# A change in five places of a hybrid encoder layer: conv-norm stores by GpSimd, its means as fp32r products, the ninth tile of values in two products, the first weight load by ScalarE

## The chip, the cores and the metric

One core of a Trainium2 chip runs the whole layer. TensorE (PE in the profile) multiplies, VectorE (DVE), ScalarE (ACT) and GpSimd (POOL) compute element by element, and SyncE (SP) issues most of the transfers. Each engine works through its own list of instructions in order. An instruction waits for the semaphores of what it needs, and everything behind it on that engine waits with it. The metric is the device time of one execution in microseconds (us); lower is better. A profiled execution also gives the span from the first to the last instruction.

## The reference, cut to what matters

A layer takes 1024 frames of a prompt and 32 frames of a running stream, 1056 rows in all, with 1024 features each:

```
p = x @ w_in                    # split into: GLU pair | q | k | v | forget logits | gate logits
u = a * sigmoid(b)              # GLU pair, 512 channels
y = causal depthwise conv, width 31, over u
y = silu(LayerNorm over the 512 channels of (y + b_dw))    # the conv norm
y_conv = y @ w_conv_out
o = forgetting attention(q, k, v, cumulated log forget gates), 8 heads of 64
m = sigmoid(g_conv) * y_conv + sigmoid(g_attn) * (o @ w_attn_out)
x1 = LN1(alpha * x + m @ w_o)
x2 = LN2(alpha * x1 + relu(x1 @ w_up)^2 @ w_down)
```

The new rows of u, k, v and log f are outputs too. Everything is fp32.

## The kernel before, in words

**Products.** An fp32 number is split into a high part (a copy in the type fp32r, made by ScalarE) and a low part (the difference, made by VectorE). A dense product is then three products of the parts: high by high, high by low, low by high (`dense` and `mm3`, recorded by `mm`, L206). Weights come in halves through a ring `raw`, and are split into `whi` and `wlo` (class `Weights`: `load`, `split`, `take`). The rows of x are kept split in `xh0..7` and `xl0..7`, with 128 features on the partitions and 1056 columns each, worked on as three chunks of 352 columns.

**Start.** `x_stream` loads weights (`raw`) and x (`xr`, two features' tiles a piece) by the SP queue and splits them. TensorE first runs 19 products that nobody reads (`keep_warm`, tile `ps_warm`), and some more between the first products of `ps_glub`, where it would wait for x.

**Stages.** First the GLU pairs (`glua`, `glub`), then the values (`ps_v`: nine tiles of 128 rows, in two halves of 260 columns; the ninth covers rows 928 to 1055 and only its last 32 are used), then q and k, then 16 tiles of gates (`ps_g`, 24 products to a chunk). Six of the gate tiles run in the first part of the kernel, which has eight PSUM banks for them. The other ten are filler in the attention stage, which has two banks for them (`bbank`). ScalarE empties a bank by copying it to `gt`; the copy is then stored to `g_s`.

**The conv norm** (`conv`) runs beside this on VectorE and ScalarE: 31 taps for each of four channel tiles, then sums of the channel tiles (`lns`), means and variances by a product with the constant matrix `mean_c` (`ps_mu_c`, `ps_var_c`, three blocks of 362 columns), `rstd_c` and a reciprocal for each block, and then twelve pieces (three blocks by four channel tiles). A piece is scaled (VectorE), passed through a sigmoid (ScalarE, `csig`), multiplied (VectorE), split into high (ScalarE, `csh`) and low (VectorE, `csl`), and both parts are stored to `s_s` by the SP queue. The third block's rows are cut in two, so its stores are two each. The y products read `s_s` much later, in the attention stage.

**Order.** Engines' lists come from running this code with an estimate of every instruction's time (class `Issue`): `conv` is a generator that is advanced between groups of products when its next step is due by that estimate. `MARGIN` says how long a product with `mean_c` waits after its sums. At the end of the first part, `I.flush()` writes out whatever of `conv` is left.

**Attention.** Its tiles reuse the memory of the first part. Head 0 is loaded by GpSimd's queue (`load_head`, `queue = nc.gpsimd if h == 0`), behind three memsets of GpSimd's (`k2`, `q2`, called `k` and `q` in the profile); other heads are loaded by SP. The first scores, `ps_s`, need all of head 0's k and q. After them the kernel goes on with gates, attention, the y products, w_o and its norm, the feed-forward products (`ps_u`, `ps_d`, `ps_dn`) and the last norm.

## Time and profile before

| what | value |
| --- | --- |
| median of 3 runs | 1446.77 us (1445.07 to 1447.04) |
| the profiled execution's own time | 1445.13 us |
| its span | 1443.0 us |
| TensorE busy | 1427.9 us, 99% of the span |
| VectorE busy | 1121.0 us, 78% |
| ScalarE busy | 679.1 us, 47% |
| GpSimd busy | 124.5 us, 9% |
| gates tiles before attention | 245.3 to 318.1 us |
| the first scores | 334.31 us |

All times of instructions below count from the span's start. A row of the timeline gives start, length, engine, line of the kernel, operation, what is written `<-` what is read, how many, and in brackets how long the engine had been idle and what ended that. The chain of waits follows the work that ended last, in order of time.

### The profile page before, as it was taken

The numbers are of one execution on the slowest core, as the hardware profiler recorded it, in microseconds if no ns is written. First come the engines' busy times: TensorE is split into PE (matmuls) and PEld (weight loads), VectorE is DVE, ScalarE is ACT, GpSimd is POOL, SyncE is SP. The second block draws the span as 40 slices with busy tenths as digits, with TensorE's granted clock in tenths as the row PEclk, the third lists the DMA queues.
The fourth block names the chain that finished last, engine by engine and source line by source line (L and its number), as shares of the span: only waits on it lengthen the run. The fifth ranks groups of instructions, "written<-read, shape, count | busy, mean of one in ns | idle before, by whom it ended". The sixth has DMA issues, their size and how long they took to land.

```text
span 1443.0 us, 28013 instructions
## 1 busy us (share of the span) xinstructions
PE 1427.9 (99%) x10643; PEld 1406.3 (97%) x10643; DVE 1121.0 (78%) x1927; ACT 679.1 (47%) x1426; POOL 124.5 (9%) x183
## 2 busy tenths in 40 slices
PE   9999999999999999999999999999999999999996
PEld 8999999999999999999999999999999999999996
DVE  6999899875666555756697888889876799889668
ACT  5113433455656556533245666676657323322134
POOL 0000000023455533000000000000000000000000
PEclk9999999999999999999999999999999999999998
DMA  7125454278455557425243348766689999894212
GB/s 247 48 61 160 159 171 167 85 244 233 120 150 147 155 146 260 152 93 182 85 138 120 131 152 295 249 241 230 228 283 342 340 321 330 270 324 179 67 45 77
DMA packets 157441, 267.91 MB, mean 186 GB/s; under 512 B 22680, under 2 KB 81272, under 8 KB 157308
## 3 DMA queue, kind: packets, MB, share of 16 engines
q1 hardware_dynamic: 156492, 264.24, 55.0%
q0 software_dynamic: 544, 1.59, 0.5%
q8 instruction: 84, 1.38, 0.4%
q14 instruction: 49, 0.40, 0.1%
q10 hardware_dynamic: 272, 0.29, 0.1%
HBM read 168.29 MB, written 97.74 MB: 184 GB/s over the span
## 4 chain that ended last, share of the span: by engine, by line
PE 97%; DVE 1%; ACT 0%; DMA 0%; issue 0%; SPq 0%; DVEq 0%
PE ps_u L206 18%; PE ps_d L206 17%; PE ps_g L206 13%; PE ps_o L206 6%; PE ps_dn L206 6%; PE ps_up L206 5%; PE ps_v L206 4%; PE ps_yc L206 3%; PE ps_k L206 3%; PE ps_glua L206 3%; PE ps_q L206 3%; PE ps_glub L206 3%; PE ps_yo L206 3%; PE ps_s L206 3%; PE ps_pv L206 2%; PE ps_tr L210 2%
## 5 line engine op out<-in xcount | busy, mean ns | idle before, releaser
L235 DVE SCALAR_TENSOR_TENSOR ca<-u,prm,ca 128x1086 f32<-128x1086 f32 x120 | 161.8, 1348 | 2.4
L206 PE MATMUL ps_g<-xh,whi 128*128 128x352 f32 x384 | 131.8, 343 | 0.0
L218 ACT ACTIVATE swhi<-s 128x512 fp32r<-128x512 f32 x100 | 61.9, 624 | 148.2 <-DVE s L227 139.8
L206 PE MATMUL ps_g<-xh,wlo 128*128 128x352 f32 x384 | 123.8, 322 | 0.0
L206 PE MATMUL ps_g<-xl,whi 128*128 128x352 f32 x384 | 121.5, 322 | 0.0
L206 PE MATMUL ps_u<-tl,swhi 128*128 128x264 f32 x416 | 118.4, 285 | 0.0
L206 PE MATMUL ps_u<-th,swhi 128*128 128x264 f32 x416 | 118.2, 284 | 0.0
L206 PE MATMUL ps_u<-th,swlo 128*128 128x264 f32 x416 | 118.2, 284 | 0.0
L218 ACT ACTIVATE whi<-raw 128x512 fp32r<-128x512 f32 (+1 forms) x120 | 69.7, 624 | 68.6 <-PE ps_glua L206 21.8
L227 DVE TENSOR_TENSOR tl<-ps_tr,th 128x512 fp32r<-128x512 f32 (+2 forms) x96 | 51.5, 553 | 60.1 <-ACT th L218 59.4
L206 PE MATMUL ps_d<-hu_h,swhi 128*128 128x264 f32 x480 | 93.0, 285 | 0.0
L206 PE MATMUL ps_d<-hu_l,swhi 128*128 128x264 f32 x480 | 92.8, 285 | 0.0
L218 ACT ACTIVATE r<-r 128x528 f32<-128x528 f32 (+1 forms) x120 | 73.9, 615 | 37.8 <-DVE r L227 35.5
L227 DVE TENSOR_TENSOR r<-r,ps_u 128x528 f32<-128x528 f32 x91 | 62.7, 701 | 29.5 <-PE ps_u L206 29.5
L227 DVE TENSOR_TENSOR wlo<-raw,whi 128x512 fp32r<-128x512 f32 (+1 forms) x100 | 64.9, 687 | 23.5 <-ACT whi L218 21.6
L206 PEld LDWEIGHTS ps_u<-th,swhi 128*128 128x128 f32 x416 | 78.3, 188 | 0.0
L206 PEld LDWEIGHTS ps_u<-th,swlo 128*128 128x128 f32 x416 | 78.3, 188 | 0.0
L206 PEld LDWEIGHTS ps_u<-tl,swhi 128*128 128x128 f32 x416 | 78.2, 188 | 0.0
L227 POOL TENSOR_TENSOR acc<-acc,lnrest 128x288 f32<-128x288 f32 x4 | 3.0, 796 | 856.7 <-ACT lnrest L218 856.7
L206 PEld LDWEIGHTS ps_d<-hu_h,swhi 128*128 128x128 f32 x480 | 74.6, 189 | 0.3 <-issue 0.2
L206 PEld LDWEIGHTS ps_d<-hu_l,swhi 128*128 128x128 f32 x480 | 74.6, 189 | 0.0
L206 PEld LDWEIGHTS ps_g<-xh,whi 128*128 128x128 f32 x384 | 72.7, 189 | 0.8
(424 smaller groups left out, 5005.5 us busy)
## 6 DMA issues: line engine op xcount, KB each, us to landing
h_s<-sp SPq DMA_DIRECT2D x84, 528.0 KB
raw<-in_w_in_dram SPq DMA_DIRECT2D x64, 256.0 KB
hu_h<-h_s SPq DMA_DIRECT2D x30, 528.0 KB
hu_l<-h_s SPq DMA_DIRECT2D x30, 528.0 KB
sraw<-in_w_up_dram SPq DMA_DIRECT2D x52, 256.0 KB
hu<-h_s SPq DMA_DIRECT2D x24, 528.0 KB
sraw<-in_w_ds_dram SPq DMA_DIRECT2D x48, 256.0 KB
g_s<-gt SPq DMA_DIRECT2D x48, 176.0 KB
```

The costliest lines, as they stand in the source:

```text
L206: self.nc.tensor.matmul(ps, lhsT=w, rhs=x, start=start, stop=stop)
L210: self.nc.tensor.transpose(ps, x, ident)
L218: self.nc.scalar.activation(out, in_, func, **kw)
L227: (self.nc.vector if eng == "dve" else self.nc.gpsimd).tensor_tensor(out, a, b, op)
L235: self.nc.vector.scalar_tensor_tensor(out, a, s, b, op0, op1)
```

## The change

- The two parts of a conv-norm piece now lie in one tile `cs` (two parts by 362 columns, a ring of four), and are stored by one transfer each (two for the third block), issued by GpSimd. `s_s` is laid out to match.
- The sums of the conv norm are split into fp32r parts too, in tiles of the same ring: one more ScalarE copy and one more VectorE subtraction for each of the six sums. A mean is then two fp32r products with `mean_c`, now of type fp32r, in place of one fp32 product.
- The ninth tile of values takes only the 32 rows it needs, with the high and low parts side by side as 64 columns of the stationary operand (`xs`, written by 16 ScalarE copies). One product with `whi` and one with `wlo` for each of the eight feature tiles takes the place of three; ScalarE and VectorE then add the two halves of the result.
- The first weight half is loaded by ScalarE's queue, ahead of its first activation; the second weight half is split after the second piece of x, not after the first; the fill-in products among the first `ps_glub` products become 2 and 1, from 5 and 2.

```
-    s_s = [tc.dram_tile([NJ, P, T], F32, name=f"s{i}_s") for i in range(2)]
+    s_s = tc.dram_tile([NJ, 2, P, T], F32, name="s_s")
...
-    act(tiny, eps, AF.Sigmoid)
...
-            W.load()
+            W.load(nc.scalar)
+            act(tiny, eps, AF.Sigmoid)
             issue()
             issue()
             W.load()
...
             W.split()
             for i in range(4 * NCH):
-                if i == 1:
+                if i == 2:
                     W.split()
...
-        mean_c = pv_.tile([P, P], F32, name="mean_c")
-        nc.gpsimd.memset(mean_c, 1.0 / C_CONV)
+        mean_c = pv_.tile([P, P], F32R, name="mean_c")
+        nc.gpsimd.memset(f32(mean_c), 1.0 / C_CONV)
...
-                    keep_warm({1: 5, 3: 2}.get(k, 0))
+                    keep_warm({1: 2, 3: 1}.get(k, 0))
...
                 for t in src[2:]:
                     tt(a, a, t, ADD)
-                return a
+
+                parts = pv_.tile([P, 2, CC], F32R, tag="cs", bufs=4, name=f"cs_{kind}{c}")
+                parts = [parts[:, 0], parts[:, 1]]
+                act(parts[0], a, AF.Copy)
+                tt(parts[1], a, f32(parts[0]), SUB)
+                return parts
...
-                mm(mu, mean_c, sums[c], True, True)
+                for i, a in enumerate(sums[c]):
+                    mm(mu, mean_c, a, i == 0, i == 1)
...
-                mm(var, mean_c, sums[c], True, True)
+                for i, a in enumerate(sums[c]):
+                    mm(var, mean_c, a, i == 0, i == 1)
...
-                    hi, lo = (pv_.tile([P, CC], F32R, tag=x, bufs=4, name=f"{x}{c}_{j}") for x in ("csh", "csl"))
+                    both = pv_.tile([P, 2, CC], F32R, tag="cs", bufs=4, name=f"cs{c}_{j}")
+                    hi, lo = both[:, 0], both[:, 1]
                     act(hi, z, AF.Copy)
                     tt(lo, z, f32(hi), SUB)
-                    for dst, src in ((s_s[0][j], hi), (s_s[1][j], lo)):
-                        if c < 2:
-                            dma(dst[:, blocks[c]], src)
-                        else:
-                            e = SEQ - 2 * CC
-                            dma(dst[:, 2 * CC:SEQ], src[:, :e])
-                            dma(dst[:, SEQ:T], src[:, CC - DEC:])
+                    dst = s_s[j].rearrange("i p t -> p i t")
+                    if c < 2:
+                        dma(dst[:, :, blocks[c]], both, nc.gpsimd)
+                    else:
+                        e = SEQ - 2 * CC
+                        dma(dst[:, :, 2 * CC:SEQ], both[:, :, :e], nc.gpsimd)
+                        dma(dst[:, :, SEQ:T], both[:, :, CC - DEC:], nc.gpsimd)
...
+        xs = pa.tile([P, 2, CH], F32R, tag="xr", bufs=XB, name="xs").rearrange("p a x -> p (a x)")
+        xs = xs[:, :2 * KD * DEC].rearrange("p (k x) -> p k x", k=KD)
+        for k in range(KD):
+            for i, t in enumerate((xh, xl)):
+                act(xs[:, k, i * DEC:(i + 1) * DEC], f32(t[k][:, SEQ:T]), AF.Copy)
...
+                    for n, (x, *w2) in enumerate(terms):
+                        for i, w in enumerate(w2):
+                            mm(ps[0:2 * DEC], x, w, n == i == 0, n == KD - 1 and i == 1)
+                        I.service()
+                    both = pa.tile([P, 2, CH], F32, tag="xr", bufs=XB, name=f"xs_{half}")
+                    both = [both[:DEC, i, :VW] for i in range(2)]
+                    for i in range(2):
+                        act(both[i], ps[i * DEC:(i + 1) * DEC], AF.Copy)
+                    tt(both[0], both[0], both[1], ADD)
```

The change also moves instructions, since the estimates of the conv norm are other ones. A row of an engine's list gives the line, the operation, and what is written and read.

TensorE, around the third product of variances, before (`ps_g_0_85` is the tenth of the 18 chunks of gates that come before attention):

```order
L206 MATMUL ps_g_0_85_3132<-xh_144,whi_2756 128x352
L206 MATMUL ps_g_0_85_3132<-xl_152,whi_2756 128x352
L206 MATMUL ps_g_0_85_3132<-xh_144,wlo_2757 128x352
L206 MATMUL ps_var_c_86_3151<-lns_v_3061,mean_c 128x362
L206 MATMUL ps_g_0_85_3132<-xh_145,whi_2756 128x352
```

and in the changed kernel (`ps_g_1_89` is the fourteenth chunk):

```order
L206 MATMUL ps_g_1_89_3281<-xh_138,whi_2859 128x352
L206 MATMUL ps_g_1_89_3281<-xl_146,whi_2859 128x352
L206 MATMUL ps_g_1_89_3281<-xh_138,wlo_2860 128x352
L206 MATMUL ps_var_c_90_3288<-cs_v_3153,mean_c 128x362 x2
L206 MATMUL ps_g_1_89_3281<-xh_139,whi_2859 128x352
```

Before, 234 products of gates stand ahead of it; now 318 do. The first scores stand behind 534 products of gates in both, and 432 of these are the 18 chunks.

ScalarE, from the copy of the eighteenth chunk (`ps_g_2_94`) on, before (`gt_0_3617` copies the first chunk of the attention stage's gates, `ps_g_0_3592`, and the third of these chunks, `ps_g_2_3648`, writes the bank that this copy empties):

```order
L218 ACTIVATE gt_2_3515<-ps_g_2_94_3478 128x352
L218 ACTIVATE whi_3518<-raw_3250 128x512
L218 ACTIVATE whi_3518<-raw_3254 128x512
L218 ACTIVATE csig_3_3529<-ca_261,prm 128x362
L218 ACTIVATE csh_2_3532<-ca_260 128x362
L218 ACTIVATE csh_3_3541<-ca_261 128x362
L218 ACT_TABLE_LOAD
L218 ACTIVATE tiny<-eps 128x1
L218 ACTIVATE gt_0_3617<-ps_g_0_3592 128x352
```

and in the changed kernel, the last rows ahead of the same `gt_0_3617`:

```order
L218 ACTIVATE csig_1_3517<-ca_258,prm 128x362
L218 ACTIVATE cs_0_3520<-ca_257 128x362
L218 ACTIVATE csig_2_3526<-ca_259,prm 128x362
L218 ACTIVATE cs_1_3529<-ca_258 128x362
L218 ACTIVATE csig_3_3535<-ca_260,prm 128x362
L218 ACTIVATE cs_2_3538<-ca_259 128x362
L218 ACTIVATE cs_3_3544<-ca_260 128x362
L218 ACT_TABLE_LOAD
L218 ACTIVATE tiny<-eps 128x1
L218 ACTIVATE gt_0_3617<-ps_g_0_3592 128x352
```

Before, two high parts of pieces (`csh_2`, `csh_3`) stood between the copy of the eighteenth chunk and `gt_0_3617`. Now seven do: the four of the third block shown here, and the last three of the second block, which follow the eighteenth chunk's copy and its two `whi`.

GpSimd, between its first memsets and the second head's, before:

```order
L827 MEMSET k_0_3563 64x1088
L829 MEMSET q_0_3565 64x1024
L830 MEMSET q_0_3565 2x1024
L201 DMA k_0_3568<-kh_s 64x1024 x2
L201 DMA q_0_3569<-qh_s 64x1024
L201 DMA q_0_3569<-ql_s 64x1024
L201 DMA k_0_3563<-kl_s 64x1024
L201 DMA k_0_3563<-c_s 2x8x128
L201 DMA q_0_3565<-qh_s 64x1024
L201 DMA q_0_3565<-c_s 2x8x128
```

and in the changed kernel, from the last four stores to the first of head 0's loads:

```order
L201 DMA s_s<-cs_2_3538 128x2x300
L201 DMA s_s<-cs_2_3538 128x2x32
L201 DMA s_s<-cs_3_3544 128x2x300
L201 DMA s_s<-cs_3_3544 128x2x32
L852 MEMSET k_0_3563 64x1088
L854 MEMSET q_0_3565 64x1024
L855 MEMSET q_0_3565 2x1024
L201 DMA k_0_3568<-kh_s 64x1024 x2
```

Sixteen stores now stand in GpSimd's list ahead of the memsets and of head 0's loads.

More of the change, by code (lines that the diff above doesn't have):

```diff
@@ L327, in __init__, with load @@
             self.engine, self.limit = "dve", NWO + 1
-        def load(self):
+        def load(self, queue=None):
             i = len(self.raw)
@@ L334, in load @@
             n = w.shape[1] // 2
-            dma(self.raw[i][:, :n], w[:, i % 2 * n:(i % 2 + 1) * n])
+            dma(self.raw[i][:, :n], w[:, i % 2 * n:(i % 2 + 1) * n], queue)
         def split(self):
@@ L636, in conv @@
             for c in range(3):
[L637 removed]
+                yield (MARGIN, sums[c])
                 mu = bank(f"mu_c{c}")[:, :CC]
[L639 removed]
+                for i, a in enumerate(sums[c]):
+                    mm(mu, mean_c, a, i == 0, i == 1)
                 sq = []
@@ L744, in hybrid_layer @@
             for t in range(9):
-                tk = slice(t * P, (t + 1) * P) if t < 8 else slice(T - P, T)
+                tk = slice(t * P, (t + 1) * P)
                 ps = bank("v")[:, :VW]
@@ L749, in hybrid_layer @@
                     wh, wl = (w[:, (k % 4) * VW:(k % 4 + 1) * VW] for w in ws[k // 4])
-                    terms.append((xh[k][:, tk], xl[k][:, tk], wh, wl))
-                dense(ps, terms)
+                    terms.append((xh[k][:, tk], xl[k][:, tk], wh, wl) if t < 8 else (xs[:, k, :], wh, wl))
                 r = P if t < 8 else DEC
-                ps = ps[P - r:P, :]
+                if t < 8:
+                    dense(ps, terms)
+                else:
+                    for n, (x, *w2) in enumerate(terms):
[7 more added lines that the diff above has]
+                    tt(both[0], both[0], both[1], ADD)
+                    ps = both[0]
                 v32 = pa.tile([P, 256], F32, tag="v32", bufs=2, name=f"v32_{half}_{t}")
-                act(v32[:r], ps[:, 0:256], AF.Copy)
-                act(zt[0:r, t, 4 * half:4 * half + 4], ps[:, 256:VW], AF.Copy)
+                act(v32[:r], ps[0:r, 0:256], AF.Copy)
+                act(zt[0:r, t, 4 * half:4 * half + 4], ps[0:r, 256:VW], AF.Copy)
                 vs = pa.tile([P, 4, P], F32R, tag="vs", bufs=2, name=f"vs_{half}_{t}")
@@ L922, in load_s @@
                     for i, t in enumerate(("sh", "sl")):
-                        dma(yr[t][k][:, cs], s_s[i][k, :, cs])
+                        dma(yr[t][k][:, cs], s_s[k, i, :, cs])
         def early():
```

3 lines of the change are left out of this document (1 added, 2 removed).

## The prediction

> **What bounds the kernel now.** I read the page's busy shares first, then its chain of work that ended last, then that chain in order of time.
>
> ```profile
> PE 1427.9 (99%) x10643; PEld 1406.3 (97%) x10643; DVE 1121.0 (78%) x1927; ACT 679.1 (47%) x1426; POOL 124.5 (9%) x183
> ...
> PEclk9999999999999999999999999999999999999998
> ...
> PE 97%; DVE 1%; ACT 0%; DMA 0%; issue 0%; SPq 0%; DVEq 0%
> ```
>
> TensorE is busy for 99% of the span and makes up 97% of the chain. So a product taken out is worth its spacing, and nothing that other engines do counts until TensorE has to wait for it. The same holds the other way: a wait that TensorE gets here has almost no idle time later to vanish in. The chain in order of time gives the prices of products:
>
> ```profile
> 9.82 2.77 PE ps_glub L206 x16
> 100.71 51.65 PE ps_v L206 x432
> 285.83 0.61 PE ps_var_c L206 x2
> 286.44 48.03 PE ps_g L206 x300
> 334.48 0.61 PE ps_s L206 x6
> ```
>
> A product of values costs 51.65 / 432 = 0.120 us, one of gates 48.03 / 300 = 0.160 us, and a mean (one fp32 product, which shows as two) 0.61 us. From the last variances to the first scores TensorE runs 300 gate products without a gap. The timeline of that stretch shows how narrow this was:
>
> ```profile
> 323.15 0.51 ACT L218 ACTIVATE csh<-ca 128x362 fp32r<-128x362 f32 x1 [1.11 <-DVE ca L235]
> 323.67 1.28 ACT L218 ACT_TABLE_LOAD   x1
> 325.08 0.45 ACT L218 ACTIVATE gt<-ps_g 128x352 f32<-128x352 f32 x1
> 323.69 0.54 DVE L227 TENSOR_TENSOR csl<-ca,csh 128x362 fp32r<-128x362 f32 x1 [0.57 <-ACT csh L218]
> 325.57 0.43 PE L206 MATMUL ps_g<-xh,whi 128*128 128x352 f32 x1
> ```
>
> After the last piece of the conv norm ScalarE loads a table and copies the first filler chunk of gates out of its bank, from 325.08 to 325.53. The third filler chunk writes that bank, and TensorE began it at 325.57. So the conv norm's end was already just in time.
>
> **Part by part: what TensorE saves.** At the start:
>
> ```profile
> 0.73 1.28 ACT L218 ACT_TABLE_LOAD   x1 [0.73 <-PEq L1933]
> 0.74 0.40 SPq L201 DMA_DIRECT2D raw<-in_w_in_dram  x1
> 1.20 0.94 SPq L201 DMA_DIRECT2D xr<-in_x_dram  x2
> 3.94 0.63 ACT L218 ACTIVATE whi<-raw 128x512 fp32r<-128x512 f32 x1 [1.71 <-DMA raw<-in_w_in_dram]
> 5.60 0.96 DVE L227 TENSOR_TENSOR xl<-xr,xh 128x352 fp32r<-128x352 f32 x2 [0.30 <-ACT xh L218]
> 7.54 0.69 DVE L227 TENSOR_TENSOR wlo<-raw,whi 128x512 fp32r<-128x512 f32 x1 [0.98 <-ACT whi L218]
> 8.15 2.70 DVE L227 TENSOR_TENSOR xl<-xr,xh 128x352 fp32r<-128x352 f32 x6
> ```
>
> Without the first weight load SP issues x 1.20 - 0.74 = 0.46 us earlier. With the second split moved back, VectorE need not sit for 0.98 us before `xl` of the second piece. TensorE waits here for `xl`, so at least 0 and at most 0.46 + 0.98 = 1.4 us are saved; I take 1.0. ScalarE's own issue of the load (SP's took 0.40) delays its table load, which then ends at 0.73 + 0.40 + 1.28 = 2.4; the weights were there at 3.94, so it costs nothing. The fill-in products left out stand where TensorE waits: 0 too.
>
> Values: 16 of 48 products of the two ninth tiles go, 16 x 0.120 = 1.9 us. That a stationary operand of 64 columns changes the spacing no row shows; between no change and none of the gain (0 to 1.9) I take 1.9, because 260 and 352 moved columns cost 0.120 and 0.160, the same per column. The 16 copies `xs` and the other additions are hidden by ScalarE's idle time in that stage, here with the busy times of PE, its weight loads, DVE and ACT:
>
> ```profile
> 100.70:152.35 51.65, 51.65 (x434) 51.65 (x433) 47.69 (x55) 17.37 (x57) 0.00 (x0) 1.00 0.51 153
> ```
>
> ScalarE works 17.37 of 51.65 us, and eight banks stand between it and TensorE; without that cover some 20 copies would cost about 0.2 us each.
>
> Means: two fp32r products cost 2 x 0.160 x 362 / 352 = 0.33 us, so each of six saves 0.28, 1.7 us together. Sum: 1.0 + 1.9 + 1.7 = 4.6 us, all before the first scores.
>
> **What the later conv norm costs.** The moved order counts more. By the orders shown above the last variances stand behind 318 gate products, not 234. In the old time TensorE came to product 318 at 286.44 + 84 x 0.160 = 299.9; take off 1.0 + 1.9 and what five new means (1.65) save on six old ones (3.66), and it is there at 295.0. Before, it ran the last variances at 285.83. Then come `rstd`, a reciprocal, and the pieces. Their pace and the pace around a weight split are in the timeline:
>
> ```profile
> 286.48 0.56 ACT L218 ACTIVATE rstd_c<-ps_var_c,eps 128x362 f32<-128x362 f32 x1 [2.06 <-PE ps_var_c L206]
> 301.96 0.60 ACT L218 ACTIVATE csig<-ca,prm 128x362 f32<-128x362 f32 x1 [0.82 <-DVE ca L235]
> 302.99 0.54 DVE L227 TENSOR_TENSOR csl<-ca,csh 128x362 fp32r<-128x362 f32 x1 [0.62 <-ACT csh L218]
> 305.16 0.54 DVE L227 TENSOR_TENSOR csl<-ca,csh 128x362 fp32r<-128x362 f32 x1 [0.62 <-ACT csh L218]
> 307.54 1.15 ACT L218 ACTIVATE whi<-raw 128x512 fp32r<-128x512 f32 x2
> 311.11 0.54 DVE L227 TENSOR_TENSOR csl<-ca,csh 128x362 fp32r<-128x362 f32 x1 [0.62 <-ACT csh L218]
> 318.12 0.46 ACT L218 ACTIVATE gt<-ps_g 128x352 f32<-128x352 f32 x1 [0.54 <-PE ps_g L206]
> ```
>
> A piece takes 305.16 - 302.99 = 2.17 us: it passes between VectorE and ScalarE, and each waits for the other. The copy of the eighteenth chunk started at 318.12; TensorE is now done with it 4.6 us earlier, so 313.5, and with the sixteenth, 48 products before, at 305.8. In ScalarE's list the sixteenth's copy (0.46) precedes the sigmoid of the third piece, at 306.2; a low part starts 302.99 - 301.96 = 1.03 after a sigmoid, so the second piece's starts at 307.2 and the fifth's, three paces later, at 313.8. Then comes the eighteenth's copy, at 313.7, its `whi` at 314.1, and the sixth low part 311.11 - 307.54 = 3.57 after that, at 317.7. Five more at 2.17 make 328.5, and the last, which has no next sigmoid beside it, 1.6 more: it starts at 330.1 and ends at 330.6, against 323.69 and 324.2 before. This end hangs on TensorE's place in the list, not on how busy ScalarE or VectorE are.
>
> First wait: from the last low part to the third filler chunk it took 325.57 - 323.69 = 1.88 us, so TensorE goes on at 332.0. It would have been there at 325.57 - 4.6 = 321.0. That is a wait of 11.0 us for ScalarE's copy.
>
> Second wait: head 0 now stands behind the last store in GpSimd's list. Before, GpSimd did its memsets and loads early:
>
> ```profile
> 286.56 1.00 POOL L827 MEMSET k<- 64x1088 f32 x1 [284.84 <-PE ps_var_c L206]
> 289.40 1.21 POOL L201 DMA_DIRECT2D k<-kh_s  x2
> 292.11 0.62 POOL L201 DMA_DIRECT2D k<-c_s  x1
> 292.71 0.54 POOL L201 DMA_DIRECT2D q<-qh_s  x1
> 293.23 0.61 POOL L201 DMA_DIRECT2D q<-c_s  x1
> 294.86 0.32 SPq L201 DMA_DIRECT2D s_s<-csh  x1
> 334.31 0.33 PE L206 MATMUL ps_s<-k,q 128*128 128x128 f32 x2
> ```
>
> and the transfers of these rows landed, by the page's list of issues (last column: us to landing), in
>
> ```profile
> k<-kh_s POOLq DMA_DIRECT2D x2, 256.0 KB, 3.8
> q<-c_s POOLq DMA_DIRECT2D x1, 8.0 KB, 6.9
> ```
>
> So the memsets took 289.40 - 286.56 = 2.84 us, and from the first load's issue to the last landing went 293.23 + 6.9 - 289.40 = 10.7 us. That GpSimd started 45 us before the scores hid it all. Now: last low part 330.6, two stores, memsets, loads. A store's issue by GpSimd with 256 rows is not in this trace; 64 rows of 4 KB cost 0.54 and 16 rows 0.62, so it does not grow with rows here, and I take 0.6 (bounds: SP's 0.32 for a store of 128 rows, and four times 0.54, or 2.2). 330.6 + 1.2 + 2.84 + 10.7 = 345.4. TensorE is at the first scores 334.31 - 325.57 = 8.7 us after 332.0, at 340.7, so it waits another 4.7 us. What is queued behind in GpSimd's list, the second head's memsets and a weight split, comes 11 us or more later too, and so do the products that need it.
>
> The first scores move from 334.31 to 345.4: +11.1 us, with the gains already in it (4.6 gained, 11.0 + 4.7 waited). After them TensorE's list is the same. The profiled execution took 1445.13 us, 2.1 more than its span of 1443.0; 1443.0 + 11.1 + 2.1 = 1456.2. The median of the runs is 1.6 us above the profiled one, so I predict **1458 us**.
>
> **Rivals.**
>
> *Only the bank counts.* The loads land while TensorE is still at the filler. For it: the first landed 3.8 us after issue, and 293.23 + 3.8 - 289.40 = 7.6 would bring the end to 342.3, near 340.7. Against it: the last of the eight took 6.9, and the second head's loads now run beside them. It gives 340.7 - 334.31 = +6.4: 1453.2 us. The Trainium skill, "DMA: Bandwidth & Descriptors" (Anatomy of one DMA — SWDGE (gpsimd) path), fits 2.0 us plus the bytes over 436 KB per us; by that estimate a 256 KB load lands in 2.6 us, which would give this case. The trace's 3.8 to 6.9 speak against it.
>
> *The stores' issue grows with rows.* At 2.2 us each, eight stores of the third block take 17.6 us from the end of the first of its low parts on (317.7 + 3 x 2.17 + 0.54 = 324.8), so they end at 342.4 and not 331.8: 10.6 us more, 1468 us. For it only the four times longer list of rows, against it the two rows above.
>
> *TensorE restarts slowly after a wait.* The row of the first fill-in products and that of the later five:
>
> ```profile
> 1.19 4.11 PE L542 MATMUL ps_warm<-warm 128*128 128x256 bf16 x19 [1.19 <-DVE warm L537]
> 6.88 0.72 PE L542 MATMUL ps_warm<-warm 128*128 128x256 bf16 x5
> ```
>
> 4.11 / 19 = 0.22 us against 0.72 / 5 = 0.14, the last one's tail included: the first products after idle ran at little over half pace for some 4 us. After the first wait that is hidden in the second (340.7 becomes 343); after the second it would cost about 2 us: 1460. The profile's granted clock reads 0.9 or more in all slices but the last and shows none of it. The Trainium skill, "TensorE: Matmul & The Clock Gate" (Part 1), says that the clock halves after an idle window of about 3.4 us and comes back after a busy one. By that rule both waits would do it. The slow first products agree; no row here shows a restart in the middle.
>
> *The waits do not arise, and the gain stands*: 1446.8 - 4.6 = 1442.2, faster. The mechanism is that the pieces keep up with TensorE. The point from which it decides: the last low part must start by 321.0 - 1.9 = 319.1. From the eighteenth chunk's copy at 313.7 seven pieces would have to take under 0.8 us each; the trace has 2.17 in every undisturbed one. It also needs GpSimd to pass head 0's loads ahead of the stores, which its list excludes. That the edits do not do what they say (64 columns cost as much as three products) only takes 1.9 us off the gain.
>
> **How the numbers follow.** Both waits as worked out: 0.59. Only the bank: 0.13. Slow restart: 0.12. Growing stores: 0.10. Waits not there: 0.06. The range reaches below the bank alone (1453.2) and short of the growing stores: 1452 to 1466. About 3 us, 0.2%, is what can be told from no change here. All cases but the last are slower by more: 0.94; the last is faster (0.04), or the same where part of a wait stays (0.02).
>
> **What would show it.** In the changed profile: TensorE idle for about 11 us near 321 before a `ps_g` product, released by ScalarE's `gt`; idle again for about 5 us near 341 before `ps_s`, released by a load of k or q; the last low part of the conv norm near 330; GpSimd's memsets right behind it; first scores near 345. For the gains: `ps_v` with 416 products in 49.7 us, pairs of means at 0.33 us, `ps_glua` starting about 1 us earlier. I am wrong if the first scores come by 336, or if the last low part lies before 320.

## The result, and the profile after

The changed kernel takes 1467.57 us (median of 4, 1466.83 to 1467.97), the kernel before 1446.07 us (median of 4 beside it): 21.5 us more, a ratio of 1.0149 with a 95% interval of 1.0137 to 1.0161. The forecast was 1458 us, with a range of 1452 to 1466: slower for the reasons given, but by almost twice as much, and above the range.

The page of the changed kernel, its busy time of TensorE, the clock and the chain that ended last:

```profile
PE 1430.8 (98%) x10623; PEld 1409.5 (96%) x10623; DVE 1124.6 (77%) x1935; ACT 685.9 (47%) x1452; POOL 135.9 (9%) x199
...
PEclk9999999997999999999999999999999999999998
...
PE 93%; DVE 2%; DMA 2%; ACT 1%; issue 1%; POOL 1%; DVEq 0%; POOLq 0%; ACTq 0%
```

TensorE's share of the chain fell from 97% to 93%, and one slice of the 40 has a clock of 0.7. What TensorE waited for, longest first (us in total, times, longest), and then the timeline of the stretch:

```profile
PE ps_g L206 <- ACT gt L218: 10.8, 2, 9.8
PE ps_s L206 <- DMA q<-c_s: 4.6, 1, 4.6
PE ps_s L206 <- DMA q<-ql_s: 4.2, 1, 4.2
```

```profile
315.46 0.43 PE L206 MATMUL ps_g<-xh,whi 128*128 128x352 f32 x1 [0.94 <-ACT gt L218]
...
331.31 0.54 DVE L227 TENSOR_TENSOR cs<-ca,cs 128x362 fp32r<-128x362 f32 x1 [0.57 <-ACT cs L218]
...
332.70 0.80 ACT L218 ACTIVATE gt<-ps_g 128x352 f32<-128x352 f32 x2
...
333.20 0.66 PE L206 MATMUL ps_g<-xh,whi 128*128 128x352 f32 x1 [9.84 <-ACT gt L218]
...
348.59 0.45 PE L206 MATMUL ps_s<-k,q 128*128 128x128 f32 x1 [4.25 <-DMA q<-ql_s]
353.68 0.45 PE L206 MATMUL ps_s<-k,q 128*128 128x128 f32 x1 [4.64 <-DMA q<-c_s]
```

Both forecast waits are there, at the places and with the releasers that were named: 9.84 us before the third filler chunk, for `gt` behind the conv norm's last piece, and then 4.25 + 4.64 us at the first scores, for head 0. The first scores that have all of head 0 start at 353.68, 19.4 us later than the 334.31 of before.

GpSimd's list between the two waits, and the landing of three of its loads (last column, us from issue):

```profile
331.32 3.02 POOL L201 DMA_DIRECT2D s_s<-cs  x4 [2.11 <-issue]
335.03 0.73 POOL L201 DMA_DIRECT2D s_s<-cs  x1 [0.70 <-issue]
335.81 1.00 POOL L852 MEMSET k<- 64x1088 f32 x1
...
338.66 1.07 POOL L201 DMA_DIRECT2D k<-kh_s  x2
...
342.51 0.62 POOL L201 DMA_DIRECT2D q<-c_s  x1
```

```profile
k<-kh_s POOLq DMA_DIRECT2D x2, 256.0 KB, 5.4
...
k<-kl_s POOLq DMA_DIRECT2D x1, 256.0 KB, 9.5
...
q<-c_s POOLq DMA_DIRECT2D x1, 8.0 KB, 11.0
```

The last low part ends at 331.85, the last store's issue at 335.76, and the last load lands at 342.51 + 11.0 = 353.5. Each of these steps is longer than forecast.

Last, the same stretch in windows (columns: busy time of PE, its weight loads, DVE, ACT and POOL, granted clock, DMA share, GB/s):

```profile
333.00:338.00 5.00, 4.80 (x16) 4.80 (x17) 0.00 (x0) 0.50 (x2) 4.08 (x6) 0.50 0.65 208
338.00:344.00 6.00, 6.00 (x38) 6.00 (x38) 0.00 (x0) 1.97 (x4) 5.88 (x10) 0.99 0.78 198
...
354.00:360.00 6.00, 6.00 (x27) 5.06 (x27) 3.40 (x11) 1.97 (x7) 0.00 (x0) 0.61 0.57 189
```

After each wait TensorE runs at a clock of 0.5 to 0.6 for about 5 us: 16 products in the first 5 us after the first wait, against 38 in the next 6.

So four amounts are to be explained: the first wait, GpSimd's stores, the landing of head 0, and the slow restart. As before, the first scores stand behind 534 products of gates.

### The profile page after: what moved, and what is told of

Same layout as the page of the kernel before. It is cut to its first block, busy times and chain, and to the rows that moved or that the text cites. A ratio compares the mean times of both kernels' runs of the same rounds, so it can differ in the third digit from the quotient of the medians.

```text
span 1466.2 us, 27978 instructions
## 1 busy us (share of the span) xinstructions
PE 1430.8 (98%) x10623; PEld 1409.5 (96%) x10623; DVE 1124.6 (77%) x1935; ACT 685.9 (47%) x1452; POOL 135.9 (9%) x199
## 4 chain that ended last, share of the span: by engine, by line
PE 93%; DVE 2%; DMA 2%; ACT 1%; issue 1%; POOL 1%; DVEq 0%; POOLq 0%; ACTq 0%
PE ps_u L206 18%; PE ps_d L206 16%; PE ps_g L206 11%; PE ps_o L206 6%; PE ps_dn L206 6%; PE ps_up L206 5%; PE ps_v L206 3%; PE ps_glub L206 3%; PE ps_yc L206 3%; PE ps_k L206 3%; PE ps_glua L206 3%; PE ps_q L206 3%; PE ps_yo L206 3%; PE ps_s L206 3%; PE ps_pv L206 2%; PE ps_tr L210 2%
```

## The experiments

### Each wait has its own part of the change

Two kernels undo one part each, a third both. First the stores go back to SP's queue, still one transfer per tile:

```
-                        dma(dst[:, :, blocks[c]], both, nc.gpsimd)
+                        dma(dst[:, :, blocks[c]], both)
...
-                        dma(dst[:, :, 2 * CC:SEQ], both[:, :, :e], nc.gpsimd)
-                        dma(dst[:, :, SEQ:T], both[:, :, CC - DEC:], nc.gpsimd)
+                        dma(dst[:, :, 2 * CC:SEQ], both[:, :, :e])
+                        dma(dst[:, :, SEQ:T], both[:, :, CC - DEC:])
```

> The changed kernel with its conv-norm stores issued by SP again, still one transfer per tile; everything else as changed. Theory (two waits in a row, each with its own cause): the wait before ps_s for head 0's loads goes, since GpSimd can load head 0 long before; the wait of about 10 us before the third filler chunk of gates stays, because the means' place in TensorE's list is unchanged. First scores at about 344 us (333.2 + 11.0, with the slow products after the wait), +10 on before: 1456 us. Rival (the stores by GpSimd also delay the conv norm itself, through the ring of cs tiles that they hold): the first wait shrinks too, first scores below 340, 1451 us or less.

Measured: 1454.67 us, ratio 1.0058 (1.0041 to 1.0075). The wait for head 0 is gone, the first wait is unchanged, and the first scores start at 344.2. TensorE's longest wait in this kernel:

```profile
PE ps_g L206 <- ACT gt L218: 10.7, 2, 9.8
```

The rival falls: the conv norm's last low part starts at 331.3 as in the changed kernel, so the stores did not hold the conv norm back. GpSimd's issue of the stores costs 1467.57 - 1454.67 = 12.9 us: the first scores come 9.5 us earlier, and the restart behind them is no longer slow.

Then the means go back to one fp32 product each, of sums that are not split, while GpSimd keeps the stores:

```
-                parts = pv_.tile([P, 2, CC], F32R, tag="cs", bufs=4, name=f"cs_{kind}{c}")
-                parts = [parts[:, 0], parts[:, 1]]
-                act(parts[0], a, AF.Copy)
-                tt(parts[1], a, f32(parts[0]), SUB)
-                return parts
+                return a
...
-                for i, a in enumerate(sums[c]):
-                    mm(mu, mean_c, a, i == 0, i == 1)
+                mm(mu, mean_c, sums[c], True, True)
```

> The changed kernel with its means as single fp32 products of unsplit sums again; stores stay with GpSimd. The last variances then stand behind 252 gate products instead of 318. Theory (the place of the means makes the first wait, GpSimd's list the second): the last low part of the conv norm starts near 324.5, the first wait is 3 us or less, TensorE would be at the first scores near 335; stores end 3.9 after the last low part, memsets 2.85, loads 14.9 to the last landing: first scores near 346 to 349, a wait of 11 to 14 us before ps_s: 1459 to 1461 us. Rival (the loads were late only because the second head's loads of SP ran beside them): they land in 10.7, first scores near 343, 1455 us.

Measured: 1462.01 us, ratio 1.0109 (1.0094 to 1.0124), 1 us above the theory's range. Its waits, and the issue of GpSimd's last store:

```profile
PE ps_s L206 <- DMA q<-ql_s: 9.2, 1, 9.2
PE ps_s L206 <- DMA q<-c_s: 5.1, 1, 5.1
...
PE ps_g L206 <- ACT gt L218: 0.8, 1, 0.8
```

```profile
328.73 0.73 POOL L201 DMA_DIRECT2D s_s<-cs  x1 [4.11 <-DMA g_s<-gt]
```

The first wait shrinks to 0.8 us, and the second grows to 14.3 us: TensorE waits at the scores for what it no longer waits for at the filler. That is why this part, undone alone, gives back only 5.6 us. GpSimd adds to it: the last low part ends at 322.57, but the last two stores were issued after 1.1 and 4.1 us of idle time, the last until 329.46. That is 6.9 us behind the low part, against 3.9 in the changed kernel; why is taken up below with the stores. Head 0's loads took from 332.36 to the scores at 347.51, 15.1 us, about as in the changed kernel (14.9).

Both undone together leave the ninth tile of values, the start, and one transfer per tile.

> The changed kernel with stores by SP and means as fp32 products; what stays of the change is the ninth tile of values, the start and one transfer per tile. TensorE comes to the third filler chunk about 2 us earlier than before, but the last variances stand behind 252 gate products, not 234. Theory (the conv norm's end hangs on the place of the last variances in TensorE's list): it ends where it did or 1 us later, so a wait of 2 to 3 us appears and the gain is lost: 1446 to 1448 us. Rival (the conv norm follows TensorE and the 2 us are kept): 1444 us.

Measured: 1445.08 us, ratio 0.9995 (0.9985 to 1.0004), no difference to before, whose median in this comparison was 1445.47. The two parts cost 1467.57 - 1445.08 = 22.5 us together, which is the whole loss within the scatter of the runs. TensorE comes to the third filler chunk at 323.7, 1.9 us earlier than before, waits 0.77 us, and starts the first scores at 333.2, 1.1 us earlier. The time lies between the theory (1446 to 1448) and the rival (1444). The theory's reason does not hold: the conv norm's last low part starts at 322.6, 1.1 us earlier than before, although the last variances stand 18 gate products later in the list. The chain that ended last shows what it followed: it stays on TensorE's gates until 304.55, goes on with ScalarE's copy of their bank and a weight split, and only then with the pieces. TensorE's earlier coming moved those too. The next runs ask what else makes the conv norm late.

### What makes the conv norm late

The forecast held that the conv norm's end hangs on the place of the last variances in TensorE's list. The planner's margin moves that place and leaves the work as it is (stores by SP here):

```
-                yield (MARGIN, sums[c])
+                yield (0.0, sums[c])
```

> The changed kernel with stores by SP, and the margin that its planner leaves between the sums and their means set from 3000 to 0 for the conv norm alone. The means stay two fp32r products; the last variances stand behind 270 gate products, not 318. Theory (the place in TensorE's list decides the first wait): the last low part comes up to 48 x 0.160 = 7.7 us earlier than 331.3, near 324, the first wait is 2 to 3 us and the first scores are near 336: 1448 us. Rival (VectorE and ScalarE were already late with the sums, so an earlier place only moves TensorE's wait to the variances): the last low part stays near 330, and 1455 us.

Measured: 1452.96 us, ratio 1.0047 (1.0032 to 1.0062), a first wait of 7.4 us. The last product of the variances starts 6.5 us earlier than in the changed kernel (289.5 against 296.0), and the last low part only 2.2 us earlier (329.1). VectorE's end of the sums for the third block's variance, before the change, in the changed kernel, and here:

```profile
280.29 1.18 DVE L227 TENSOR_TENSOR lns_v<-lns_v,sq_c 128x362 f32<-128x362 f32 x2
```

```profile
290.47 0.54 DVE L227 TENSOR_TENSOR cs_v<-lns_v,cs_v 128x362 fp32r<-128x362 f32 x1 [0.57 <-ACT cs_v L218]
```

```profile
288.92 0.54 DVE L227 TENSOR_TENSOR cs_v<-lns_v,cs_v 128x362 fp32r<-128x362 f32 x1 [0.63 <-ACT cs_v L218]
...
292.18 4.69 DVE L239 RECIPROCAL rstd_c<-rstd_c 128x362 f32<-128x362 f32 x2 [1.10 <-ACT rstd_c L218]
296.79 1.22 DVE L227 TENSOR_TENSOR wlo<-raw,whi 128x512 fp32r<-128x512 f32 x2
297.93 2.41 DVE L239 RECIPROCAL rstd_c<-rstd_c 128x362 f32<-128x362 f32 x1
```

VectorE ends the sums at 281.5, 291.0 and 289.5. So it is 8 us late even at the earlier place, and the last low part and the time are nearer to the rival's than to the theory's. Each of six sums now has a subtraction of 0.54 us that stands right behind ScalarE's copy and waits some 0.6 us for it: 6 x (0.54 + 0.6) = 6.9 us, most of the 8. And with margin 0 a weight split (`wlo`) lands between the second and third reciprocal. The chains that ended last show how the two causes lie beside each other. In the changed kernel the chain stays on TensorE's gates until 305.12, where a weight split follows and then the pieces: there the place in TensorE's list decides. With margin 0 it leaves TensorE at 275.4 and runs over VectorE and ScalarE alone until 331.0: there their work decides, and it gives an end only 2.2 us earlier than the place did. The place itself moved because of that work: with unsplit sums and the same margin the last variances stand behind 252 gate products, with split sums behind 318.

To take that work from VectorE, the next kernel has GpSimd subtract, on the base of stores by SP and margin 0 (the planner then puts the last variances behind 258 gate products, not 270):

```
-                tt(parts[1], a, f32(parts[0]), SUB)
+                tt(parts[1], a, f32(parts[0]), SUB, "pool")
```

> The changed kernel with stores by SP, margin 0 for the conv norm's means, and the low parts of the six sums computed by GpSimd instead of VectorE. Theory (the first wait comes from VectorE: each split of a sum costs its list 0.54 us and about 0.6 of waiting for ScalarE's copy, some 6.9 us for six, and so its last sum ended at 290.95 instead of 281.5; the place of the means in TensorE's list only followed): VectorE ends the last sum near 284, the last low part of the conv norm comes near 323 to 324, the first wait is 1 to 4 us, 1444 to 1447 us. Rival (the place in TensorE's list decides; it is 258 products here, 270 in the run with margin 0): first wait 5 us or more, 1451 us.

Measured: 1448.83 us, ratio 1.0019 (1.001 to 1.0028), between the two forecasts. VectorE and the first wait:

```profile
281.62 1.18 DVE L227 TENSOR_TENSOR lns_v<-lns_v,sq_c 128x362 f32<-128x362 f32 x2
...
286.70 4.69 DVE L239 RECIPROCAL rstd_c<-rstd_c 128x362 f32<-128x362 f32 x2 [1.10 <-ACT rstd_c L218]
292.05 1.29 DVE L227 TENSOR_TENSOR wlo<-raw,whi 128x512 fp32r<-128x512 f32 x2 [0.65 <-ACT whi L218]
293.26 2.41 DVE L239 RECIPROCAL rstd_c<-rstd_c 128x362 f32<-128x362 f32 x1
```

```profile
PE ps_g L206 <- ACT gt L218: 5.4, 1, 5.4
```

The sums end at 282.8, 6.7 us earlier than with VectorE's subtraction, so that much of the theory is shown. But the first wait, 5.4 us, is on the rival's side. The weight split is still between the reciprocals, where before the three ran together (284.69 to 291.65): 0.65 us of waiting and 1.2 us of work. The last low part starts at 325.1 and not at 323 to 324, and TensorE, which now has all its gains, comes at 321.6. What is left can be taken from the pace of the twelve pieces, 2.17 us each here too. VectorE's low part of a piece is issued one piece later, so that it finds ScalarE's copy finished:

```
-            late = None
-            for piece in pieces + [None]:
+            late = later = None
+            for piece in pieces + [None, None]:
...
+                split = None
                 if late:
...
                     act(hi, z, AF.Copy)
+                    split = c, j, z, both
+                if later:
+                    c, j, z, both = later
+                    hi, lo = both[:, 0], both[:, 1]
                     tt(lo, z, f32(hi), SUB)
...
+                later = split
```

> The run with sums split by GpSimd, stores by SP and margin 0, and in the conv norm's pieces VectorE's low part of a piece taken one piece later, so that it does not wait 0.61 us for ScalarE's copy of the same piece. Theory (the pace of 2.17 us a piece is a chain between VectorE and ScalarE; without the wait it is 1.6 to 1.75): the last low part is 4 to 5 us earlier, near 319, TensorE never waits before the third filler chunk, and all gains of the change show: 1.9 for values, 1.7 for means and about 0.3 for the start: 1442 to 1443 us. Rival (VectorE and ScalarE are simply full there): pace 2.0 or more, 1444 to 1446 us.

Measured: 1441.29 us, ratio 0.9962 (0.9947 to 0.9977): faster than both kernels, by 4.2 us against before and 26.3 us against the changed one, and 0.7 us below the theory's range. VectorE's low parts of two consecutive pieces, and TensorE's longest waits:

```profile
298.57 0.53 DVE L227 TENSOR_TENSOR cs<-ca,cs 128x362 fp32r<-128x362 f32 x1
...
300.03 0.53 DVE L227 TENSOR_TENSOR cs<-ca,cs 128x362 fp32r<-128x362 f32 x1
```

```profile
PE ps_warm L542 <- DVE warm L537: 1.2, 1, 1.2
PE ps_s L206 <- ACT p L218: 0.6, 1, 0.6
```

The pace is 1.46 us wherever no weight split comes between, the last low part starts at 318.0, and TensorE waits for no `gt`. First scores come at 329.80, 4.5 us earlier than before. That is about what the change's own gains make, which a conv norm in time lets through: 1.95 for values, 1.65 for means and 0.6 for the start in this profile, 4.2 us.

The same one-piece delay was put on the kernel with fp32 means, to see its part alone.

> The run with fp32 means and stores by SP (1445.1 us, a wait of 0.8 before the third filler chunk), and the low part of a piece taken one piece later. Theory: the wait of 0.8 goes, the conv norm ends 4 to 5 us earlier, and what is kept is 1.9 for values and 0.3 for the start: 1443.5 to 1444.3 us, about 1.5 us more than the run with split sums. Rival (no gain, since 0.8 us was all that the end of the conv norm cost): 1444.5 to 1445 us.

Measured: 1447.71 us, ratio 1.0012 (1.0002 to 1.0021); slower than both forecasts. The first scores do come early, at 327.96, but the planner now puts them behind 510 gate products and not 534, so a chunk of 24 (3.8 us) moves behind them, and TensorE has new waits in the attention stage:

```profile
PE ps_tr L210 <- DVE tl L227: 2.2, 3, 1.6
```

From the first scores to the first y products TensorE idles 3.9 us, against 0.4 before. The chunk and the waits together use up the gain: the y products start at 549.2, 1.0 us later than before. The measured time is 2.2 us longer than before; what the other 1.2 us are stays open. The run says that the gain of the run before is that of the whole combination, in the order that its planner made.

### Why head 0 came so late

The landing was first to be freed from the second head's loads by placing these later in the code.

```
-                    if i == 2:
+                    if i == (4 if n == 0 else 2):
                         load(n + 1)
```

> The changed kernel with the second head's loads placed two rows of scores later in SP's list, behind more stores of gates; head 0's loads by GpSimd are untouched. Theory (head 0's loads landed late because SP loaded the second head beside them, DMA at 260 GB/s in that stretch): from the first of them to the last landing it takes about 10.7 us as before the change, not 14.9, and the first scores that need c_s come 4 us earlier than 353.7: 1463 to 1464 us. Rival (these loads are slow in GpSimd's own queue, which runs its eight transfers one after the other): the last landing stays 14 to 15 us after the first issue, 1467 us.

Measured: 1466.67 us, ratio 1.0141 (1.0124 to 1.0158). It decides nothing: SP's loads of the second head did not move behind head 0's but started earlier, at 333.8 us and not at 337.7, and head 0 took 13.6 us from its first issue to the scores. A second attempt holds them by data: VectorE writes a column of the second head's tiles behind the first scores.

```
+            if h == 1:
+                for t in (k1, q1, k2[0:DH], q2[0:DH], v[:, 0]):
+                    nc.vector.memset(f32(t[:, 0:1]), 0.0)
             queue = nc.gpsimd if h == 0 else None
```

> The changed kernel, with one column of the second head's k, q and v tiles set to zero by VectorE behind the second row of scores, and loaded over afterwards: so SP cannot load the second head before TensorE has its first scores. (The run before this, with these loads later in the code, left them at 333.8 to 344.6 us: SP's list did not move them behind head 0's.) Theory (the two queues share the DMA engines: GpSimd's took 0.42 to 0.71 of them at 342 to 352 us, SP's 0.32 to 0.63, while before GpSimd's had them nearly to itself): head 0 lands about 11 us after its first issue instead of 14.9, the first scores that need c_s start near 350 instead of 353.7; the total is uncertain, since the second head comes later. Rival (GpSimd's own queue is the slow one): 14 to 15 us from the first issue to the last landing, first scores at 353 or later.

Measured: 1463.02 us, ratio 1.011 (1.0095 to 1.0125). The issues and the scores of this kernel:

```profile
338.21 1.07 POOL L201 DMA_DIRECT2D k<-kh_s  x2
...
342.06 0.61 POOL L201 DMA_DIRECT2D q<-c_s  x1
...
348.38 0.44 PE L206 MATMUL ps_s<-k,q 128*128 128x128 f32 x1 [2.49 <-DMA q<-c_s]
```

Its last load landed 6.2 us after issue instead of 11.0, and 10.1 us after the first issue instead of 14.9; before it was 10.7. The theory holds: the loads are late because SP loads the second head beside them. The queues in the windows from first issue to last landing show the same, before and in the changed kernel (packets, MB, share of the 16 DMA engines; `software_dynamic` is GpSimd's queue):

```profile
q0 software_dynamic: 544, 1.59, 61.2%
q1 hardware_dynamic: 687, 0.89, 26.6%
```

```profile
q1 hardware_dynamic: 799, 2.06, 55.2%
q0 software_dynamic: 544, 1.59, 42.4%
```

GpSimd's queue moved the same 1.59 MB in 10.7 and in 14.8 us; SP's moved 0.89 MB beside it before and 2.06 MB after. In the run with the held loads it was 0.58 MB beside and 10.1 us.

For the stores, the four narrow ones of the third block were given to SP:

```
-                        dma(dst[:, :, SEQ:T], both[:, :, CC - DEC:], nc.gpsimd)
+                        dma(dst[:, :, SEQ:T], both[:, :, CC - DEC:])
```

> The changed kernel with the four narrow stores of the third block (32 columns) issued by SP instead of GpSimd; the twelve wide ones stay with GpSimd. Theory (GpSimd's queue takes no further store while too many are under way, which is the 2.11 and 0.70 us of idle time before stores that nothing explains, and each store costs 0.72): GpSimd ends its last store one issue after the last low part, 331.85 + 0.73 = 332.6 instead of 335.76, and head 0 comes 3 us earlier: 1464.5 us. Rival (the idle time is a wait for a part of cs that the profile names wrongly): it stays, and only four issues of 0.72 go, most of them beside the pieces: 1466.5 us.

Measured: 1463.63 us, ratio 1.0121 (1.0106 to 1.0136). The last of GpSimd's stores in this kernel:

```profile
332.27 0.73 POOL L201 DMA_DIRECT2D s_s<-cs  x1 [0.89 <-DVE cs L227]
```

The last store's issue ends at 333.00 instead of 335.76, behind a wait for `cs` alone, and the first scores that have all of head 0 come at 349.76, 3.9 us earlier (of which 1.1 is a shorter landing). So the 2.1 and 0.7 us were a cost of GpSimd's queue and not a late part of `cs`.

The landings of the single stores say more. In the changed kernel the store issued at 326.32 landed after 4.7 us, at 331.0, and the late one, three stores behind it, was issued at 331.32. In the run with fp32 means the store issued at 321.36 took 7.1 us, until 328.5, and the one three behind it was issued at 328.73. The same holds in three more of these kernels (the two on the second head's loads, and that of the next section): a late store is issued about 0.3 us after the store three before it has landed. So no store went out while three others were under way. It is not a limit of three transfers as such, since all eight of head 0's loads, of 64 and 16 rows, were issued by 343.1, before the first landed at 343.7. A limit on rows (three stores have 768, the eight loads 416) would fit both, but no run tests it.

### The slow restart

84 bf16 products that nobody reads fill TensorE's wait for head 0:

```
                 I.fill(k1, k2, q1, q2, ps)
+                if self.h == 0 and self.r == ROWS[0]:
+                    for _ in range(84):
+                        nc.tensor.matmul(ps[:, 0:256], lhsT=ident_b, rhs=bfs[:, 0:256], start=True, stop=True)
```

> The changed kernel with 84 bf16 products that nobody reads (256 columns, into the bank of the first scores) ahead of the first scores, so that TensorE does not idle while head 0 is on its way. Theory (the first 5 us of products after a wait run at half pace, which costs 2.3 us after the second wait): these products take 84 x 0.11 = 9.2 us inside the 9 us of waiting, the gates after the scores run at 0.16 us at once, and everything from there on comes 2.3 us earlier: 1465.2 us. Rival (the slow products come from operands that arrive late, or from the loads running beside them, and not from the idle time): no gain, 1467.5 us.

Measured: 1465.79 us, ratio 1.0135 (1.012 to 1.015). By the times alone, 1.8 us less is within the two intervals; the trace shows it. The window that had a clock of 0.61 and 27 products:

```profile
354.00:360.00 6.00, 6.00 (x42) 5.45 (x42) 4.92 (x15) 3.76 (x12) 0.00 (x0) 1.00 0.79 245
```

The first scores that have all of head 0 start some 0.2 us earlier than in the changed kernel, and the first group of four `ps_s` products at 357.21 and not 359.75, 2.5 us earlier: some 2.3 us were the restart. The transfers beside it were not fewer (a DMA share of 0.79 in this window, against 0.57), so idle time, not the loads, made the products slow.

### The start

> The kernel before with the start of the change alone: first weight half by ScalarE's queue, second split after the second piece of x, 2 and 1 fill-in products in place of 5 and 2. Theory (the earlier loads land no earlier, because weights and x now load at once, and fewer fill-ins leave TensorE slow for longer): ps_glua and ps_v start within 0.2 us of before, and the time is that of before, 1445 to 1447 us. Rival (my forecast): ps_v starts 1.0 us earlier, at 99.7; since the conv norm was just in time, no more than that shows in the time.

This is the kernel before with the queue of the first weight half, the later second split and the fewer fill-ins, and nothing else. Measured: 1445.51 us, ratio 0.9997 (0.9988 to 1.0006). The copy of the first weight half and the first values, before and with the new start:

```profile
3.94 0.63 ACT L218 ACTIVATE whi<-raw 128x512 fp32r<-128x512 f32 x1 [1.71 <-DMA raw<-in_w_in_dram]
...
L206 PE MATMUL ps_v<-whi,xh x144: 278/282/292, 100.5 to 151.8; 128*128 128x260 f32 x144
```

```profile
4.51 0.63 ACT L218 ACTIVATE whi<-raw 128x512 fp32r<-128x512 f32 x1 [1.81 <-DMA raw<-in_w_in_dram]
...
L206 PE MATMUL ps_v<-whi,xh x144: 278/282/292, 100.3 to 151.5; 128*128 128x260 f32 x144
```

The weights are issued at 0.73 us, as before, and land 0.6 us later, with x's loads beside them from 0.74 on and not from 1.20; `ps_v` starts 0.2 us earlier, not 1.0.

## Why the prediction was right or wrong

Its mechanism was right: two waits in a row, the first at the third filler chunk for `gt` behind a later conv norm, the second for head 0 behind the stores in GpSimd's list. Undoing the split means left 0.8 us of the first wait, and undoing the stores by GpSimd took away the second. What failed are sizes: three terms on the way that sets the end were too small or left out (the landing of head 0's loads, the stores' issue, the restart), a fourth, the end of the conv norm, was 1.2 us short, and one reason was only half right. Forecast and trace:

| step of the prediction | forecast | trace |
| --- | --- | --- |
| last low part of the conv norm starts | 330.1 | 331.3 |
| first wait | 11.0 us | 9.8 us |
| two last stores | 1.2 us | 3.9 us |
| memsets | 2.84 us | 2.85 us |
| first load's issue to last landing | 10.7 us | 14.9 us |
| products after the second wait | 0 (a rival: 2) | 2.3 us |

- *"From the first load's issue to the last landing went 10.7"*, carried over, is the largest miss: +4.2 us. It was taken from a stretch in which SP moved 0.89 MB beside; the prediction itself said that the second head's loads now run beside them, but used it only against the rival "only the bank counts". The Trainium skill, "DMA: Bandwidth & Descriptors" (Issuing engines are not separate DMA queues), says that transfers from all engines run interleaved on the same 16 DMA engines. The trace agrees, 42% and 55% of them for the two queues in these 14.8 us. The estimate of 2.6 us for a 256 KB load, which the prediction worked out from that page of the Trainium skill, does not hold here: these six loads took 5.0 to 11.2 us.
- *"A store's issue ... I take 0.6"*: 0.72 each is close. What failed is the count: only two stores were set behind the last low part, as if GpSimd kept up. GpSimd issued four stores from 331.32 on, after 2.1 us of idle time, and the last after another 0.7: +2.7 us. The rival of growing stores put 2.2 us on every store; the cost was in the queue, by the landings above a wait for earlier stores, and not in each one's issue.
- *"After the second it would cost about 2 us"*, the rival of the slow restart, was given 0.12 and happened: 2.3 us after the second wait, while the 2.4 after the first (TensorE took 11.1 us to the scores, not 8.7) was hidden, as that rival said. The prediction turned it down because the clock showed 0.9 in every slice of a profile without a wait in the middle, which is no evidence on waits.
- *"This end hangs on TensorE's place in the list, not on how busy ScalarE or VectorE are"*: the number was within 1.2 us, the reason only half right. In the changed kernel the chain does stay on TensorE until 305.12, but with the place moved back 6.5 us the end came only 2.2 us earlier, because VectorE and ScalarE then set it. The prediction's sum has no term for the six subtractions; with their waits they are about 6.9 of the 8 to 9.5 us by which VectorE's sums came late, and with the work on GpSimd the sums ended at 282.8.
- *Gains*: values 1.9 were 1.95, as 416 products in 49.70 us, and a pair of means takes 0.34 us by the gap in the chain (279.88 + 4.79 to 285.01):

```profile
100.77 49.70 PE ps_v L206 x416
...
279.88 4.79 PE ps_g L206 x30
285.01 3.83 PE ps_g L206 x24
```

  The start gave nothing here (`ps_v` at 100.77, before at 100.71) and 0.2 in its own run, where 1.0 was forecast. With that and a wait of 0.94 us at 315.46 TensorE came to the third filler chunk at 323.4 and not at 321.0, so the first wait was shorter although its end was later. That this wait is only 1.2 us off is in part luck: both its ends were later than forecast.

The sum: 11.1 forecast, +1.2 for the later conv norm, +2.7 for stores, +4.2 for landing, +2.3 for the restart make 21.5 us. That this is the measured difference to the tenth is chance. Between the two profiles the y products come 21.7 us later (569.9 against 548.2), and the feed-forward products `ps_d` too, while the spans differ by 23.2 us; the last 1.5 us arise behind these points, in work that the change does not touch, and are not explained. Each of the four terms alone would have stayed inside the range; together they do not.

## What to carry to other kernels

A duration that is carried over from a trace holds for what ran beside it: when a load is moved, ask what it will now run with, and price it at that. The list of a lightly loaded engine is a chain too: a transfer that is put on it delays whatever stands behind, and here it also waited until earlier transfers had landed. A split that an otherwise busy engine must wait for costs it the wait too (0.54 us of work was 1.15 us of VectorE's time). Where two engines pass a piece back and forth, issue the second one's part a piece later: the pace here went from 2.17 to 1.46 us, and with the sums on GpSimd and the stores on SP the products saved then showed in the time. On the kernel with fp32 means the same step gained nothing.

## What was not expected of the hardware

- GpSimd's queue stood still for 2.1 and 0.7 us between stores of 256 rows, though their data was there, until the store three before had landed (331.0, then an issue at 331.32), and did not when every second store of the third block went to SP. In the run with fp32 means, where a store took 7.1 us to land, it stood still for 4.1 us. Its issue of such a store took 0.72 us, whether 300 or 32 columns wide, against 0.54 for a load of 64 rows.
- After a wait of 9.8 us, and again after waits of 4.25 and 4.64 us with one product between, products ran at half pace for about 5 us, with a granted clock of 0.50 to 0.61. The Trainium skill, "TensorE: Matmul & The Clock Gate" (Part 1), says that the clock halves after an idle window of about 3.4 us and needs a busy one to come back. The trace agrees, at 4.9 us of half pace (333.20 to 338.05). Waits can add up to such a window: in the run with the held loads they were 2.29 and 2.49 us, with one product of 0.30 us between, and TensorE then ran 25 products in 6 us at a clock of 0.58. The price varied with the run: after a first wait of 5.4 to 9.8 us TensorE took 10.4 to 11.5 us to the scores, against 8.7 without a wait.
- At the start, where the clock reads 1.00, the products between 6.0 and 10.2 us ran at half pace in six of the thirteen profiles that have the new start (14 or 15 products in the window, against 17 to 19), with `ps_v` at 100.4 to 100.6 us instead of 99.9 to 100.3. The code of these starts is the same; why one or the other comes is open.
